# Six instead of four gate tiles in the half-size block of seven products

## The chip, the core and the metric

The kernel runs on one core of one Trainium2 chip. The time is that of the core on the device, in microseconds (us), as the median of several executions. One further execution is recorded by the hardware profiler; its span runs from the first to the last instruction. TensorE (PE) does the matmuls, VectorE (DVE), ScalarE (ACT) and GpSimd (POOL) the elementwise work; SyncE (SP) issues most DMA transfers.

## The reference

One layer of a hybrid encoder on 512 positions of width 2048, all in fp32:

```python
h = jnp.einsum('bsd,de->bse', x, w_in[layer])                 # 512 x 2048 by 2048 x 8192
qa, ka, va, ga, qb, kb, vb, gb = jnp.split(h, splits, axis=-1)  # 1024 columns each
ya = _dilated_attention(heads(qa, N_HEADS_A), heads(ka, N_HEADS_A), heads(va, N_HEADS_A), t5_bias)
yb = _neighbourhood_attention(heads(qb, N_HEADS_B), heads(kb, N_HEADS_B), heads(vb, N_HEADS_B), na_rpb[layer])
ya = merge(ya) * jax.nn.silu(ga.astype(jnp.float32))
yb = merge(yb) * jax.nn.silu(gb.astype(jnp.float32))
y = jnp.concatenate([ya, yb], axis=-1).astype(x.dtype)
out = jnp.einsum('bse,ed->bsd', y, w_out[layer])
x = _layer_norm(DEEPNORM_ALPHA * x + out, ln_gain[layer], ln_bias[layer])
```

Each group has 16 heads of 64. Group A sees keys at three dilations with a bucketed bias, group B a two-dimensional neighbourhood with its own bias. The gate paths `ga` and `gb` are 2 x 1024 columns: 16 gate tiles of 128 columns, one for each pair of heads.

## The kernel before, in words

**Precision.** Every fp32 operand is split into a high part (rounded to the type that TensorE takes at full rate, `wh` for a weight) and a low part (`wl`, the rest). A product is three matmuls: high by high, high by low, low by high. ScalarE makes the high half (an activation with Copy), VectorE the low half (a subtraction); a ring `halves` of six tiles holds three pairs, so splits run at most two units ahead of TensorE.

**Stage 1, projections.** First a plain block computes 4 gate tiles while x arrives (`plain_block`). Then `strassen_block` computes the six 1024-column projections k, q, v of the two groups, and, after the fourth of them, one more block of kind "s" with some gate tiles. Each of these blocks is a two-by-two block product done with seven products instead of eight (Strassen's method in a form with fewer additions). A product is a list of units; a unit has four steps: add two quarters of the weight where the product needs it (L371, VectorE), high half (L375, ScalarE), low half (L380, VectorE), matmuls. `run_blocks` issues for step n the addition of unit n+3, the high half of unit n+2, then the functions that hang `behind` this step (combining the products into results, storing, loading), the low half of unit n+2 and last the matmuls of unit n. The order on PE, DVE and ACT is the order in which the code is written; SP and POOL are ordered by a scheduler.

In a normal block the 1024 columns of weight are the moving operand, 512 at a time (L402 to L404). In the "s" block the weight tile is the stationary operand and 256 positions of x move (L393 to L395); the result has the gate's columns on partitions. Four quarters of the weight are loaded (`load`), four results combined (`combine_`, `last`) and passed through the gate function (`silu`: ScalarE tanh, VectorE closing) to DRAM (`sg_d`).

**Stage 2, attention.** 128 score steps n (four for each head, eight for each pair i = n // 8; pairs alternate between group A, even i, and group B, odd i). Step n does on PE: two score matmuls (L665, L666), then in two portions a number of *fillers*, and between the portions the transposes of step n-2's probabilities (L685). VectorE adds the bias and takes the maximum (L622), ScalarE exponentiates (L626); after the transposes ScalarE makes the high half `th` (L690) and VectorE the low half `tl` (L691). In every fourth step (n % 4 == 2) the eight value matmuls of the previous head (L707) read `th` and then `tl`; ScalarE copies one half (L831), VectorE adds (L832, `y`). For a pair, once in eight steps: the denominators are inverted (L843), transposed, copied by ScalarE (L720), sent to DRAM and loaded back spread over partitions as `rc` by POOL (L721, L723); six steps later VectorE multiplies by the gate (L730) and by `rc` (L738) and splits the result (L739, L740).

The **fillers** are independent matmuls that keep PE at work: first the plain gate tiles (`gate_unit`, 48 matmuls of 512 columns each, L561; each needs two weights of 128 x 1024, split in L546 and L547, and a closing L567), then the first half of the output projection (`out_first`, L755, 384 matmuls). A table gives how many fillers each of four consecutive steps takes; 49 are used before step 0, what is left is issued after the last step.

**Stage 3.** The second half of the output projection, the residual and the layer norm.

Of the kernel before, what the change touches and what calls it, by code (L numbers as in the profile page):

```python
# [25 lines left out]
HALF = 256  # L26
# [44 lines left out]
def hybrid_layer(tc, xT, xn, w_in, w_early, w_mid, w_gate, w_out, t5x, brow, rpb, cmask, eye, gain, lbias, out):  # L71
    nc = tc.nc
    from contextlib import ExitStack
    with ExitStack() as ctx:
# [19 lines left out]
        def slot(tag, dtype=F32, name=None):  # L94
            return arena.tile([128, sizes[tag[0]]], dtype, name=name or tag, tag=tag)
# [254 lines left out]
        def strassen_block(src, kind, g, hooks):  # L350

            base = len(jobs)
            units, tiles = (2, 1) if kind == "s" else (4, 2)

            def load(q, tags):
                def run():
                    for u in range(units):
                        raw = slot(tags[u], F32, "braw")
                        nc.sync.dma_start(raw, src[units * q + u])
                        raws[q].append(raw)  # L360
                return run
# [3 lines left out]
            def product(i, pool, q, other=None, onto=None):  # L365
                accs = [] if onto is None else onto
                first, skip = onto is None, onto is not None

                def add(u):
                    if other is not None:  # L370
                        nc.vector.tensor_tensor(raws[q][u], raws[q][u], raws[other][u], ALU.add)  # L371

                def high(u):
                    h = halves.next("wh", F32R)
                    nc.scalar.activation(h, raws[q][u], AF.Copy)  # L375
                    return h

                def low(u, h):
                    l = halves.next("wl", F32R)
                    nc.vector.tensor_tensor(l, raws[q][u], f(h), ALU.subtract)  # L380
                    return h, l

                def run(u, h, l):
                    if u == 0 and first:
                        accs.extend(bank(pool, "acc") for _ in range(tiles))
                    if kind == "s":
                        for kk in range(4):
                            k = 4 * u + kk
                            ah, al = operand(i, k)
                            for n in range(2):  # L390
                                c = slice(256 * kk + 128 * n, 256 * kk + 128 * n + 128)
                                o = accs[0][:, HALF * n:HALF * n + HALF]
                                nc.tensor.matmul(o, h[:, c], ah, start=first and k == 0 and n == 0, stop=False, skip_group_check=skip)  # L393
                                nc.tensor.matmul(o, h[:, c], al, start=False, stop=False, skip_group_check=skip)
                                nc.tensor.matmul(o, l[:, c], ah, start=False, stop=k == 7 and n == 1, skip_group_check=skip)  # L395
                    for t in range(2 if kind != "s" else 0):
                        for kk in range(2):
                            k = 2 * u + kk
                            ah, al = operand(i, k)
                            c = slice(512 * kk, 512 * kk + 512)  # L400
                            q = slice(128 * t, 128 * t + 128)
                            nc.tensor.matmul(accs[t], ah[:, q], h[:, c], start=first and k == 0, stop=False, skip_group_check=skip)  # L402
                            nc.tensor.matmul(accs[t], al[:, q], h[:, c], start=False, stop=False, skip_group_check=skip)  # L403
# [17 lines left out]
            def pair(name):  # L421
                if name not in made:
                    t = temps.next(name)
                    made[name] = [t[:, :512], t[:, 512:]]
                return made[name]

            p1 = product(1, pss, 0)
# [4 lines left out]
            product(3, None, 3, onto=p5)  # L432
            product(4, None, 0, 2, onto=p7)
            tags = list(sets)
            if kind == "s":
                for q, ahead, i, m in ((0, 6, 0, 0), (1, 5, 0, 2), (3, 3, 1, 0), (2, 0, 1, 2)):
                    behind.setdefault(base - ahead, []).append(load(q, tags[i][m:m + 2]))
            else:
                for q, ahead, i in ((0, 6, 0), (1, 4, 1), (3, 2, 2)):
                    behind.setdefault(base - ahead if base else -4, []).append(load(q, tags[i]))  # L440
                at(2, 2, load(2, tags[1]))

            def keep(t):
                nc.scalar.activation(pair("r1")[t], p1[t], AF.Copy)
# [27 lines left out]
            def put(name, ch, half, t):  # L472
                o = p1[t] if name == "c11" else pair(home[name])[t]
                if kind == "v":
                    store_v(g, ch, half, t, o)
                    return
                sg = vst.next("sg")[:, :512]
                silu(sg, o)
                for n in range(2):
                    nc.sync.dma_start(sg_d[EARLY + 2 * ch + n][:, HALF * half:HALF * half + HALF], sg[:, HALF * n:HALF * n + HALF])  # L480
# [324 lines left out]
        with tc.manual_schedule(engines=engines):  # L805
            prepare()
            for _ in range(3):
                close()
            while step[0] < 0:
                fill(7)  # L810
                close()
            for n in range(136):
                b, i = n % 4, n // 8
                mixing = n % 4 == 2 and 6 <= n <= 130
                amount = ((8, 6, 1, 6) if n < 64 else (8, 7, 1, 7))[b]
                if b == 0 and n < 124:
                    load_bias(n // 4 + 1)
                if n % 8 == 0 and n < 120:
                    load_kq(i + 1)
                if n % 8 == 4 and n < 128:  # L820
                    if n < 120:
                        load_v(i + 1)
                    load_sg(i)
                exponent = scores(n) if n < 128 else None
                while held:
                    held.pop(0)()
                if mixing:
                    if exponent:
                        exponent()
                    mine, theirs, y, t = values(n // 4 - 1)  # L830
                    nc.scalar.activation(t, theirs, AF.Copy)  # L831
                    nc.vector.tensor_tensor(y, mine, t, ALU.add)  # L832
# [185 lines left out]
def _weights(w_in, w_out):  # L1018
# [19 lines left out]
    mid = []  # L1038
    for i in range(2):
        for j in range(2):  # L1040
            a = np.concatenate([w[8 * i:8 * i + 8, :, c:c + 128] for c in gate[EARLY + 2 * j:EARLY + 2 * j + 2]], axis=2)
            mid.append(a.reshape(2, 4, 128, 256).transpose(0, 2, 1, 3).reshape(2, 128, 1024))
# [38 lines left out]
```

## Time and profile before

| | |
|---|---|
| time, median of 3 executions | 976.12 us (976.05 to 976.37) |
| profiled execution | 976.42 us, its span 974.6 us |
| granted TensorE clock | 0.996 of full speed on average |
| half-size block, in the span | 367.9 to 409.1 us |
| attention, first to last scores | 576.4 to about 870 us |

How to read a row: times are us from the span's start, first the start, then the duration; `wl<-braw,wh` means that tile wl is written from braw and wh; `x4` is a count of like instructions that a row merges; what stands in brackets at the end is how long the engine was idle before and what ended the wait. A row of windows has start:end, then for each engine the busy time with its count of instructions, the granted clock, the DMA engines' busy share and GB/s. In the page's slices each digit is a busy share in tenths.

### The profile page before, as it was taken

Reading aid. Unit: us, or ns where it says so; the run is one execution under the profiler, and the core shown is the slowest. Engines: PE = TensorE matmul, PEld = TensorE weight load, DVE = VectorE, ACT = ScalarE, POOL = GpSimd, SP = SyncE. Lnnn points to the kernel's source line nnn. Section 1 sums busy time; section 2 is a strip of 40 time slices with the busy share of each in tenths; the row PEclk is TensorE's granted clock in tenths of the full one; section 3 lists DMA queues with packets and bytes.
Section 4 is the critical chain, followed back from the end, with each engine's and each line's share of the span. In section 5 each row is a group of like instructions: output and inputs, shape, how many; then the busy total and the mean of one; then the engine's idle time right before and its main releaser. Section 6 shows DMA issues by size and latency. Waiting matters only on the chain.

```text
span 974.6 us, 13969 instructions
## 1 busy us (share of the span) xinstructions
PE 964.0 (99%) x4779; PEld 804.2 (83%) x4779; DVE 758.6 (78%) x1143; ACT 497.1 (51%) x858; POOL 176.5 (18%) x325
## 2 busy tenths in 40 slices
PE   8999999999999999999999999999999999999996
PEld 6887888888888889988888888888888888888885
DVE  7897778679789777796788856777876767777877
ACT  7454444444444344443445446767766666763300
POOL 1006646835642000000000000011110000100021
PEclk9999999999999999999999999999999999999998
DMA  9816796698496087420872687878877688768222
GB/s 332 280 65 133 225 329 213 171 308 220 115 334 226 22 283 204 163 96 21 265 183 96 205 273 213 226 224 228 233 229 222 195 236 214 203 223 298 87 72 102
DMA packets 119287, 194.17 MB, mean 199 GB/s; under 512 B 48479, under 2 KB 68831, under 8 KB 119216
## 3 DMA queue, kind: packets, MB, share of 16 engines
q1 hardware_dynamic: 106544, 169.67, 57.0%
q0 software_dynamic: 12096, 22.95, 8.7%
q8 instruction: 38, 0.62, 0.3%
q10 hardware_dynamic: 576, 0.66, 0.2%
q14 instruction: 33, 0.27, 0.1%
HBM read 148.68 MB, written 44.50 MB: 198 GB/s over the span
## 4 chain that ended last, share of the span: by engine, by line
PE 96%; DVE 1%; ACT 1%; DMA 1%; issue 0%; SPq 0%; DVEq 0%; ACTq 0%
PE acc L402 16%; PE acc L404 16%; PE acc L403 16%; PE acc L755 15%; PE acc L561 9%; PE pv L707 4%; PE pt L685 4%; PE sc L666 2%; PE sc L665 2%; PE pt L259 1%; PE acc L278 1%; PE acc L279 1%; PE acc L280 1%; PE sc L755 1%; PE acc L393 1%; PE acc L395 1%
## 5 line engine op out<-in xcount | busy, mean ns | idle before, releaser
L375 ACT ACTIVATE wh<-braw 128x1024 fp32r<-128x1024 f32 x182 | 193.3, 1062 | 268.6 <-PE acc L403 201.4
L380 DVE TENSOR_TENSOR wl<-braw,wh 128x1024 fp32r<-128x1024 f32 x182 | 222.7, 1226 | 52.4 <-ACT wh L375 52.1
L402 PE MATMUL acc<-wh,xk 128*128 128x512 f32 x384 | 151.5, 394 | 0.0
L404 PE MATMUL acc<-wl,xk 128*128 128x512 f32 x384 | 149.9, 390 | 0.0
L403 PE MATMUL acc<-wh,xk 128*128 128x512 f32 x384 | 149.7, 390 | 0.0
L371 DVE TENSOR_TENSOR braw<-braw 128x1024 f32<-128x1024 f32 x104 | 127.7, 1228 | 0.1
L402 PE MATMUL acc<-wh,op 128*128 128x512 f32 x288 | 113.3, 393 | 0.0
L404 PE MATMUL acc<-wl,op 128*128 128x512 f32 x288 | 112.3, 390 | 0.0
L403 PE MATMUL acc<-wh,op 128*128 128x512 f32 x288 | 112.2, 390 | 0.0
L755 PE MATMUL acc<-wh,yk 128*128 128x512 f32 x320 | 108.2, 402 | 0.0
L691 DVE TENSOR_TENSOR tl<-pt,th 128x256 fp32r<-128x256 f32 (+1 forms) x128 | 71.1, 555 | 35.8 <-ACT th L690 34.1
L690 ACT ACTIVATE th<-pt 128x256 fp32r<-128x256 f32 (+1 forms) x128 | 62.2, 489 | 47.6 <-PE pt L685 45.4
L404 PEld LDWEIGHTS acc<-wl,xk 128*128 128x128 f32 x384 | 72.1, 188 | 15.3
L402 PEld LDWEIGHTS acc<-wh,xk 128*128 128x128 f32 x384 | 72.2, 188 | 15.2 <-ACT bias L150 0.9
L403 PEld LDWEIGHTS acc<-wh,xk 128*128 128x128 f32 x384 | 72.2, 188 | 14.4
L626 ACT ACTIVATE p<-s,mn 128x512 f32<-128x512 f32 (+1 forms) x96 | 62.2, 648 | 29.0 <-DVE mn L622 28.6
L622 DVE CUSTOM_DVE_ANT_0 s<-sc,biases 128x512 f32<-128x512 f32 (+2 forms) x128 | 67.7, 529 | 10.9 <-PE sc L666 10.0
L561 PE MATMUL acc<-xk,wh 128*128 128x512 f32 x256 | 75.3, 404 | 0.0
L755 PEld LDWEIGHTS acc<-wh,yk 128*128 128x128 f32 x320 | 58.5, 189 | 8.8
L160 POOL DMA_DIRECT2D bias<-rows_d x128 | 61.3, 487 | 16.4 <-DMA bias<-rows_d 5.3
L755 PE MATMUL acc<-wl,yk 128*128 128x512 f32 x160 | 64.0, 403 | 0.0
L404 PEld LDWEIGHTS acc<-wl,op 128*128 128x128 f32 x288 | 54.1, 188 | 11.4
(185 smaller groups left out, 1707.1 us busy)
## 6 DMA issues: line engine op xcount, KB each, us to landing
braw<-in_w_in SPq DMA_DIRECT2D x96, 512.0 KB
wraw<-in_w_out SPq DMA_DIRECT2D x32, 512.0 KB
k_d<-kst SPq DMA_DIRECT2D x64, 128.0 KB
q_d<-kst SPq DMA_DIRECT2D x64, 128.0 KB
v_d<-vst SPq DMA_DIRECT2D x32, 256.0 KB
q<-q_d SPq DMA_DIRECT2D x32, 256.0 KB
wraw<-in_w_gate SPq DMA_DIRECT2D x16, 512.0 KB
k<-k_d SPq DMA_DIRECT2D x16, 512.0 KB
```

The lines of the kernel that those rows point to most:

```text
L371: nc.vector.tensor_tensor(raws[q][u], raws[q][u], raws[other][u], ALU.add)
L375: nc.scalar.activation(h, raws[q][u], AF.Copy)
L380: nc.vector.tensor_tensor(l, raws[q][u], f(h), ALU.subtract)
L402: nc.tensor.matmul(accs[t], ah[:, q], h[:, c], start=first and k == 0, stop=False, skip_group_check=skip)
L403: nc.tensor.matmul(accs[t], al[:, q], h[:, c], start=False, stop=False, skip_group_check=skip)
L404: nc.tensor.matmul(accs[t], ah[:, q], l[:, c], start=False, stop=k == 7, skip_group_check=skip)
L561: nc.tensor.matmul(acc, w[:, k * 128:k * 128 + 128], X[8 * u + k][:, s], start=u == 0 and n == 0 and k == 0, stop=u == 1 and n == 2 and k ...
L622: nc.vector.tensor_tensor_reduce(*flat, bias, 1.0, 3e38, ALU.add, ALU.min, mn)
L626: nc.scalar.activation(p[:, to:to + n].rearrange("p (b r c) -> p b r c", r=8, c=c), s[:, :n].rearrange(order, r=8, c=c), AF.Exp, bias=mn, ...
L690: nc.scalar.activation(th, pt[:, :nch], AF.Copy)
L691: nc.vector.tensor_tensor(tl, pt[:, :nch], f(th), ALU.subtract)
L755: nc.tensor.matmul(acc[:, part], yk[k][:, s, c], w[:, wk], start=first and kk == 0 and n == 0, stop=last and kk == 1 and n == 2)
```

## The change

Of the 16 gate tiles, 4 stay in the first plain block. The half-size block takes 6 instead of 4, and the fillers 6 instead of 8. In the half-size block a unit becomes 768 columns (two k-tiles of 384) where it was 1024 (four k-tiles of 256), each product has 4 units instead of 2, and its result takes two PSUM banks (512 and 256 columns) where it took one. Quarters are loaded and placed as in the normal blocks. The table of fillers goes from (8, 6, 1, 6) up to step 63 and (8, 7, 1, 7) after it to (6, 5, 1, 4) up to step 75 and (8, 6, 1, 6) after it.

```diff
-EARLY, MID = 4, 4
+EARLY, MID = 4, 6
...
-            units, tiles = (2, 1) if kind == "s" else (4, 2)
+            units, tiles = 4, 2
+            cols, wide = (128 * MID // 2, (512, HALF * (MID // 2 - 2))) if kind == "s" else (512, (512, 512))
...
-                        raw = slot(tags[u], F32, "braw")
+                        raw = slot(tags[u], F32, "braw")[:, :2 * cols]
...
                     if kind == "s":
-                        for kk in range(4):
-                            k = 4 * u + kk
+                        for kk in range(2):
+                            k = 2 * u + kk
                             ah, al = operand(i, k)
-                            for n in range(2):
-                                c = slice(256 * kk + 128 * n, 256 * kk + 128 * n + 128)
-                                o = accs[0][:, HALF * n:HALF * n + HALF]
+                            for n in range(MID // 2):
+                                c = slice(cols * kk + 128 * n, cols * kk + 128 * n + 128)
+                                o = accs[n // 2][:, HALF * (n % 2):HALF * (n % 2) + HALF]
...
-            if kind == "s":
-                for q, ahead, i, m in ((0, 6, 0, 0), (1, 5, 0, 2), (3, 3, 1, 0), (2, 0, 1, 2)):
-                    behind.setdefault(base - ahead, []).append(load(q, tags[i][m:m + 2]))
-            else:
-                for q, ahead, i in ((0, 6, 0), (1, 4, 1), (3, 2, 2)):
-                    behind.setdefault(base - ahead if base else -4, []).append(load(q, tags[i]))
-                at(2, 2, load(2, tags[1]))
+            for q, ahead, i in ((0, 6, 0), (1, 4, 1), (3, 2, 2)):
+                behind.setdefault(base - ahead if base else -4, []).append(load(q, tags[i]))
+            at(2, 2, load(2, tags[1]))
...
-                amount = ((8, 6, 1, 6) if n < 64 else (8, 7, 1, 7))[b]
+                amount = ((6, 5, 1, 4) if n < 76 else (8, 6, 1, 6))[b]
```

What moves on the engines, at three places. In the changed program the lines behind the first edits have other numbers: L394 to L396 are L393 to L395 of before, and from L480 on a line stands two lower. First PE at the first k-tile of the half-size block, before and after (acc is the PSUM bank, xk the moving half of x, wh and wl the weight's halves):

```order
L393 MATMUL acc_3306<-xk0_98,wh_3246 128x256
L394 MATMUL acc_3306<-xk0_98,wh_3246 128x256
L395 MATMUL acc_3306<-xk0_98,wl_3248 128x256
L393 MATMUL acc_3306<-xk0_98,wh_3246 128x256
L394 MATMUL acc_3306<-xk0_98,wh_3246 128x256
L395 MATMUL acc_3306<-xk0_98,wl_3248 128x256
```

```order
L394 MATMUL acc_3312<-xk0_98,wh_3250 128x256
L395 MATMUL acc_3312<-xk0_98,wh_3250 128x256
L396 MATMUL acc_3312<-xk0_98,wl_3260 128x256
L394 MATMUL acc_3312<-xk0_98,wh_3250 128x256
L395 MATMUL acc_3312<-xk0_98,wh_3250 128x256
L396 MATMUL acc_3312<-xk0_98,wl_3260 128x256
L394 MATMUL acc_3313<-xk0_98,wh_3250 128x256
L395 MATMUL acc_3313<-xk0_98,wh_3250 128x256
L396 MATMUL acc_3313<-xk0_98,wl_3260 128x256
```

Each k-tile of x now meets three weight tiles, the third in a second bank.

Next VectorE from the sum of head 2 (y) to the last low half of head 3, the cycle in which pair 0 is multiplied by rc, before and after:

```order
L832 TENSOR_TENSOR y<-pv,tmp 64x512
L691 TENSOR_TENSOR tl<-pt,th 128x256
L622 ISA s,mn<-sc,biases 128x192
L622 ISA mn 128x1
L691 TENSOR_TENSOR tl<-pt,th 128x256
L547 TENSOR_TENSOR wl<-wraw,wh 128x1024
L738 TENSOR_TENSOR y<-y,rc 128x512
L622 ISA s,mn<-sc,biases 128x512
L622 ISA mn 128x1
L691 TENSOR_TENSOR tl<-pt,th 128x256
L843 RECIPROCAL den<-den 128x8
```

```order
L830 TENSOR_TENSOR y<-pv,tmp 64x512
L689 TENSOR_TENSOR tl<-pt,th 128x256
L620 ISA s,mn<-sc,biases 128x192
L620 ISA mn 128x1
L689 TENSOR_TENSOR tl<-pt,th 128x256
L736 TENSOR_TENSOR y<-y,rc 128x512
L620 ISA s,mn<-sc,biases 128x512
L620 ISA mn 128x1
L689 TENSOR_TENSOR tl<-pt,th 128x256
L841 RECIPROCAL den<-den 128x8
```

The split of a filler's weight (wl) has left this cycle, so VectorE comes to the multiplication by rc one split earlier. In the same way the cycle of head 4 loses a gate closing (sgo).

Last SP in the steps 8 to 13, the transfers that are issued around the loading of rc for pair 0, before and after:

```order
L589 DMA ql<-q_d 64x2x512
L540 DMA wraw<-in_w_gate 128x1024
L649 DMA biases<-biasa_d 128x560
L598 DMA vv<-v_d 128x1024
L609 DMA sg<-sg_d 128x512
L540 DMA wraw<-in_w_gate 128x1024
```

```order
L587 DMA ql<-q_d 64x2x512
L538 DMA wraw<-in_w_gate 128x1024
L647 DMA biases<-biasa_d 128x560
L596 DMA vv<-v_d 128x1024
L607 DMA sg<-sg_d 128x512
```

The weight load that closed this group before has left it; the next transfer is a bias table of a later head.

More of the change, by code (lines that the diff above doesn't have):

```diff
@@ L384, in run @@
                     if u == 0 and first:
[L385 removed]
+                        accs.extend(bank(pool, "acc")[:, :n] for n in wide)
                     if kind == "s":
[L387 to L388 removed]
+                        for kk in range(2):
+                            k = 2 * u + kk
                             ah, al = operand(i, k)
[L390 to L393 removed]
+                            for n in range(MID // 2):
+                                c = slice(cols * kk + 128 * n, cols * kk + 128 * n + 128)
+                                o = accs[n // 2][:, HALF * (n % 2):HALF * (n % 2) + HALF]
+                                nc.tensor.matmul(o, h[:, c], ah, start=first and k == 0 and n % 2 == 0, stop=False, skip_group_check=skip)
                                 nc.tensor.matmul(o, h[:, c], al, start=False, stop=False, skip_group_check=skip)
[L395 removed]
+                                nc.tensor.matmul(o, l[:, c], ah, start=False, stop=k == 7 and (n % 2 == 1 or n == MID // 2 - 1),
+                                                 skip_group_check=skip)
                     for t in range(2 if kind != "s" else 0):
@@ L476, in put @@
                     return
-                sg = vst.next("sg")[:, :512]
+                sg = vst.next("sg")[:, :wide[t]]
                 silu(sg, o)
-                for n in range(2):
-                    nc.sync.dma_start(sg_d[EARLY + 2 * ch + n][:, HALF * half:HALF * half + HALF], sg[:, HALF * n:HALF * n + HALF])
+                for n in range(wide[t] // HALF):
+                    nc.sync.dma_start(sg_d[EARLY + MID // 2 * ch + 2 * t + n][:, HALF * half:HALF * half + HALF], sg[:, HALF * n:HALF * n + HALF])
             for t in range(tiles):
```

11 lines of the change are left out of this document (6 added, 5 removed).

## The prediction

> **What bounds the kernel now.** I read the page first, then the groups of instructions by form, then the order of time at two places, and last the waits.
>
> ```profile
> PE 964.0 (99%) x4779; PEld 804.2 (83%) x4779; DVE 758.6 (78%) x1143; ACT 497.1 (51%) x858; POOL 176.5 (18%) x325
> PE   8999999999999999999999999999999999999996
> PEclk9999999999999999999999999999999999999998
> ...
> PE 96%; DVE 1%; ACT 1%; DMA 1%; issue 0%; SPq 0%; DVEq 0%; ACTq 0%
> ```
>
> TensorE is busy for 99% of the span, in every slice, at the full granted clock, and the chain that ended last is 96% TensorE. So the change is worth first of all what it takes from or adds to TensorE's instruction stream, and a stall counts only if it reaches TensorE. A busy share can hide short waits, because the page says that ends of matmuls are modelled. I therefore price matmuls by the distance between starts, not by their duration.
>
> ```profile
> 403.83 0.28 PE L394 MATMUL acc<-xk,wh 128*128 128x256 f32 x1
> 403.95 0.28 PE L395 MATMUL acc<-xk,wl 128*128 128x256 f32 x1
> 404.07 0.28 PE L393 MATMUL acc<-xk,wh 128*128 128x256 f32 x1
> ...
> 367.90:409.10 41.20, 41.20 (x346) 41.20 (x345) 30.89 (x34) 18.42 (x22) 0.00 (x0) 1.00 0.64 192
> ```
>
> In the half-size block one matmul of 256 columns starts 0.12 us after the last. The window of the whole block (columns: TensorE, weight load, DVE, ACT, POOL, clock, DMA share, GB/s) holds its 336 of them and some transposes in 41.2 us, at most 0.1226 us each.
>
> ```profile
> 620.77 1.09 PE L561 MATMUL acc<-xk,wh 128*128 128x512 f32 x4
> 621.69 0.60 PE L685 MATMUL pt<-ident,p 128*128 128x128 f32 x4
> ...
> 576.88 1.98 PE L561 MATMUL acc<-xk,wh 128*128 128x512 f32 x8
> 578.70 0.39 PE L665 MATMUL sc<-k,q 128*128 128x512 f32 x1
> ```
>
> Fillers of 512 columns start 0.92/4 = 0.23 us apart between attention steps (the row's two decimals allow 0.225 to 0.235), and 1.82/8 = 0.2275 us in a longer row.
>
> **The change, part by part.**
>
> *TensorE, removed.* Two gate tiles fewer among the fillers: 2 units x 3 passes x 8 = 48 matmuls each, 96 in all, at 0.23 us: -22.1 us (-21.6 at 0.225, -22.6 at 0.235).
>
> *TensorE, added.* The half-size block had 7 products x 8 k-tiles x 2 tiles x 3 = 336 matmuls and gets 7 x 8 x 3 x 3 = 504: 168 more at 0.12 us, +20.2 us (at 0.1226 us, +20.6). Net -1.9 us, between -2.4 and -1.0. The seven products save one multiplication in eight, and much of that is eaten by 256 columns costing 0.12 us and not half of 0.2275.
>
> [...]
>
> *VectorE and ScalarE in the half-size block.* A unit shrinks from 24 to 18 matmuls, so from 24 x 0.12 = 2.9 to 18 x 0.12 = 2.16 us, with 768 columns to be added and split in it.
>
> ```profile
> L380 DVE TENSOR_TENSOR wl<-braw,wh 128x1024 fp32r<-128x1024 f32 x182 | 222.7, 1226 | 52.4 <-ACT wh L375 52.1
> L375 ACT ACTIVATE wh<-braw 128x1024 fp32r<-128x1024 f32 x182 | 193.3, 1062 | 268.6 <-PE acc L403 201.4 <-issue 29.0 <-PE acc L394 19.3
> L88 DVE TENSOR_TENSOR kst<-pt,kst 128x512 fp32r<-128x512 f32 x16 | 11.1, 691 | 16.0 <-ACT kst L87 16.0
> ```
>
> 768 columns on VectorE lie midway between 0.691 and 1.226: 0.96 us. A unit with an addition takes 2 x 0.96 = 1.92 of 2.16 us. Over the block: 28 splits and 16 additions make 42.2 us, the five combining operations and four gate closings, each on 512 and on 256 columns, about 10 us: 52 of 60.5 us, 86% against 30.89/41.2 = 75% now. The tightest place is the start of the fifth product: after the last matmul of the fourth, three combining operations on 512 columns (2.1 us) and a split stand in 2.16 us, then three on 256 columns, a gate closing and a split (about 2.9 us) in the next. Counted from the fifth product's start, the second of these splits is done at about 5.7 us, and its matmuls begin at three units, 6.5 us. Cover 0.8 us, since splits run two units ahead. Cost 0; if the cover were gone, both steps together exceed their 4.3 us by at most 1.6 us. The loads become 16 of 384 KB (6.3 MB for 4.2) in a block that is 20 us longer; the DMA share was 0.64, so 0.
>
> *Attention with fewer fillers.* Up to step 75 the fillers go from 21 (23 from step 64) to 16 in four steps: 454 - 353 = 101 fewer, 23 us less of TensorE's time; later 21 for 23, and 46 instead of 15 are left at step 128, behind which the tail has more cover than now.
>
> ```profile
> 577.10:750.60 173.50, 173.49 (x943) 144.30 (x942) 128.42 (x303) 120.10 (x284) 17.88 (x33) 1.00 0.81 226
> ```
>
> VectorE's 128.4 us lose four splits and two gate closings (4 x 1.2 + 2 x 0.7 = 6.3): 122 in 150 us, 81% instead of 74%; ScalarE 76%, from 69%. The mean fits. Single cycles of four steps might not, because TensorE is 5 x 0.23 = 1.15 us earlier at the next value products (L707), which need VectorE's last low half (tl). The fullest cycle now:
>
> ```profile
> 619.04 0.69 DVE L832 TENSOR_TENSOR y<-pv,tmp 64x512 f32<-64x512 f32 x1 [1.02 <-ACT tmp L831]
> 620.38 0.68 DVE L567 SCALAR_TENSOR_TENSOR sgo<-sgo,acc 128x512 f32<-128x512 f32 x1
> 622.18 1.22 DVE L547 TENSOR_TENSOR wl<-wraw,wh 128x1024 fp32r<-128x1024 f32 x1
> 624.53 0.68 DVE L730 TENSOR_TENSOR y<-y,sg 128x512 f32<-128x512 f32 x1
> 625.74 0.69 DVE L691 TENSOR_TENSOR tl<-pt,th 128x512 fp32r<-128x512 f32 x1
> ...
> 626.93 0.39 PE L707 MATMUL pv<-tl,vv 128*128 128x512 f32 x1
> ```
>
> VectorE runs there without a gap from 619.04 to 626.43, 0.5 us before TensorE reads tl. With the same work, 1.15 us less would stall TensorE by 0.65 us. But in the changed order the gate closing (sgo, 0.6 us) is no longer in this cycle, which leaves about nothing. Over a whole pair of group A there is more room:
>
> ```profile
> 615.10:635.10 20.00, 19.99 (x109) 16.29 (x108) 15.63 (x35) 15.38 (x35) 2.17 (x4) 1.00 0.82 217
> 635.10:650.70 15.60, 15.60 (x86) 13.03 (x86) 11.44 (x33) 10.74 (x30) 2.16 (x4) 1.00 0.84 237
> ```
>
> 15.6 of 20.0 us in the first of these stretches (group A) become about 15.0 of 17.7, 85%; the group-B stretch behind it goes from 73% to some 80%. The other cycles have one or two extras in the changed order, not three. Cost 0, bound 0.65 us in each of the nine cycles of group A, about 6 us.
>
> *What is late next: rc.* The reciprocals of the denominators go by ScalarE and POOL to DRAM and back, and VectorE waits for them in order.
>
> ```profile
> 600.23 0.25 ACT L720 ACTIVATE tmp<-pt 8x128 f32<-8x128 f32 x1
> 600.88 0.54 POOL L721 DMA_DIRECT2D rc_d<-tmp  x1 [21.50 <-ACT tmp L720]
> 605.78 0.38 SPq L540 DMA_DIRECT2D wraw<-in_w_gate  x1
> 605.83 1.07 POOL L723 DMA_DIRECT2D rc<-rc_d  x2 [3.83 <-DMA rc_d<-tmp]
> 613.42 0.69 DVE L738 TENSOR_TENSOR y<-y,rc 128x512 f32<-128x512 f32 x1 [0.58 <-DMA rc<-rc_d]
> 616.39 0.42 DVE L691 TENSOR_TENSOR tl<-pt,th 128x256 fp32r<-128x256 f32 x1 [0.66 <-ACT th L690]
> 616.87 0.64 PE L707 MATMUL pv<-tl,vv 128*128 128x256 f32 x4
> ...
> 636.06 0.25 ACT L720 ACTIVATE tmp<-pt 8x128 f32<-8x128 f32 x1
> 647.81 0.67 DVE L738 TENSOR_TENSOR y<-y,rc 128x512 f32<-128x512 f32 x1
> ...
> 673.45 0.53 POOL L721 DMA_DIRECT2D rc_d<-tmp  x1 [8.90 <-ACT tmp L720]
> 685.85 0.69 DVE L738 TENSOR_TENSOR y<-y,rc 128x512 f32<-128x512 f32 x1 [0.17 <-DMA rc<-rc_d]
> ...
> DMA to landing us min/median/max: 2.9/5.3/7.3
> ```
>
> For pair 0 rc lands 613.42 - 600.48 = 12.9 us after the ScalarE copy ended (pair 4: 12.7, counting 0.3 us to POOL), for pair 2 after at most 11.5 us, since nothing waited. At best it is the second load's issue (half of the 1.07 us behind 605.83, so 5.9 us) and the fastest landing of 2.9 us: 8.8. From VectorE's multiplication to the end of the tl behind it are 3.4 us, and TensorE reads it at 16.4 us now; ten fillers fewer on that stretch make it 14.1 us. So rc landing after 10.7 us stalls TensorE: 0 at 8.8, 2.2 us at 12.9. That can happen for the four group-A pairs with an even number up to step 75 (the others have longer steps behind them): 0 to 8.8 us. In the changed order the weight load that went out just ahead of rc (605.78 in pair 0) moves to other places, and POOL issues rc right behind rc_d, so I take it nearer to the early end: two of four late by 0.6 us, +1.2 us.
>
> *Sum.* -22.1 + 20.2 + 1.2 = -0.7 us. The profiled execution took 976.42 us, so 975.7; it lies 0.3 us above the median of 976.12, so 975.4 us by the median.
>
> **Rivals.**
>
> *A: nothing stalls.* -1.9 us, 974.2 us. For it: VectorE's work fits each cycle by the rows above, and TensorE is busy for 173.49 of 173.50 us there. Against: VectorE waited for rc three times already, and the stretch gets 14% shorter.
>
> [...]
>
> *B: rc becomes the bound of these stretches.* If the transfers take as long as in pair 0 for all four pairs, 4 x 2.2 = 8.8 us: 976.1 - 1.9 + 8.8 = 983 us. It turns the result to slower from a mean of about 1 us for each pair, a landing at 11.7 us. For it: pairs 0 and 4 show 12.9 and 12.7 us, and the same bytes have to pass in less time. Against: pair 2's 11.5 at most, with no wait.
>
> *C: VectorE bounds the half-size block and the full cycles.* 1.6 us in the block and 0.65 us in some three cycles: 976.1 - 1.9 + 3.5 = 977.7 us. Against it: idle time that the cycles still have, and 0.8 us of cover.
>
> **How the numbers follow.** What this kernel's measurement can tell from no change is 0.2%, 2 us: below 974.2 is faster, above 978.1 slower. My forecast, some stalls that eat a part of the gain: 0.50. A: 0.25, half of which falls below 974.2, as the net of TensorE alone reaches to -2.4 us. B 0.15, of which most is slower; C 0.10, a third of it slower. I add a little to faster, as the pace of removed fillers may be higher than I see: faster 0.20, same 0.62, slower 0.18. The range goes from 973.7 (-2.4, no stall) to 979.0 us (four late rc of 1.2 us each), which leaves the worse half of B out.
>
> **What would show it.** The window of the half-size block should be 61 to 62 us, its matmuls still 0.12 us apart; if longer, look whether wl or wh ended a wait of TensorE there (C). The stretch from the first scores to step 76 should shrink from 173.5 to 150-152 us with VectorE at 80%; gaps between L707 starts at the th-to-tl change show stalls, and VectorE's idle time before the multiplication by rc says whether it is rc. If rc's wait grows from 2.1 us in total to over 8, B holds. The forecast is wrong if the block or the next block's start shows waits for braw, or if fillers wait for a weight.

## The result, and the profile after

The changed kernel takes 991.38 us in the median (990.34 to 992.54, 4 executions), the kernel before on the same chip 976.23 us (976.05 to 976.37). The ratio is 1.0155, with an interval of 1.0143 to 1.0167: 1.5% slower. The forecast was 975.4 us and the range ended at 979.0. The profiled execution took 991.0 us with a span of 989.2 us, 14.6 us longer than before.

The page of the changed kernel: busy time, TensorE in 40 slices, and the chain that ended last, by engine and by line.

```profile
PE 966.9 (98%) x4851; PEld 805.7 (81%) x4851; DVE 767.3 (78%) x1168; ACT 504.7 (51%) x871; POOL 185.5 (19%) x323
PE   8999999999999999999999999989997999999996
...
PE 21%; issue 4%; DMA 3%; DVE 1%; ACT 1%; POOL 0%; DVEq 0%; ACTq 0%; POOLq 0%
PE acc L753 13%; PE pv L705 2%; PE pt L683 2%; DMA rc_d<-tmp 2%; DMA rc<-rc_d 1%; PE sc L753 1%; PE pt L753 1%; PE sc L664 1%; PE sc L663 1%; POOL rc L721 0%; DVE s L620 0%; DVE z L939 0%; DVE wl L545 0%; ACT p L624 0%; ACT wh L544 0%
```

Two of the slices that were all 9 are an 8 and a 7 now, at 643 to 668 and at 742 to 767 us. The shares of the chain add up to about 30%, so it follows only the last part of the span, and in that part the two transfers that bring `rc` now stand in it.

The windows of the half-size block and of the stretch from the first scores to step 76 (columns as in the prediction: TensorE, weight load, DVE, ACT, POOL, clock, DMA share, GB/s). The second has the same place in the program as the window 577.10:750.60 of before.

```profile
367.40:428.50 61.10, 61.10 (x510) 60.97 (x509) 49.70 (x63) 29.10 (x40) 0.00 (x0) 1.00 0.54 167
597.60:762.80 165.20, 154.77 (x842) 125.82 (x841) 121.86 (x298) 116.09 (x279) 17.79 (x33) 0.99 0.83 222
```

The block is as forecast: 61.1 us (61 to 62 were expected), without a gap on TensorE, VectorE at 49.7 us (52 expected). The attention stretch is not: it should have shrunk from 173.5 to 150 to 152 us and takes 165.2. VectorE's work in it is 121.9 us, what I had counted (122), but TensorE is idle for 165.20 - 154.77 = 10.4 us where it was idle for 0.01.

What TensorE waited for in the attention of the changed kernel, from 590 to 870 us (us in total, times, the longest). The same view of the attention before is empty.

```profile
PE pt L714 <- DVE den L841: 5.9, 3, 3.5
PE pv L705 <- ACT th L688: 4.5, 8, 1.2
```

And VectorE's wait for `rc` over the whole execution, after and then before:

```profile
DVE y L736 <- DMA rc<-rc_d: 9.0, 4, 4.7
```

```profile
DVE y L738 <- DMA rc<-rc_d: 2.1, 3, 1.3
```

By the test that the prediction set ("from 2.1 us in total to over 8") rival B holds. But TensorE does not wait for the low half behind `rc`, as rival B had it. It waits for denominators. The worst place, in order of time, first TensorE and then VectorE:

```profile
750.92 0.40 PE L753 MATMUL acc<-wl,yk 128*128 128x512 f32 x1
754.82 0.27 PE L714 MATMUL pt<-ident,den 128*8 128x128 f32 x1 [3.51 <-DVE den L841]
...
756.55 2.07 PE L705 MATMUL pv<-th,vv 128*128 128x512 f32 x4 [1.22 <-ACT th L688]
758.42 1.56 PE L705 MATMUL pv<-tl,vv 128*128 128x512 f32 x4
759.82 0.39 PE L753 MATMUL acc<-wh,yk 128*128 128x512 f32 x1
```

```profile
753.00 0.69 DVE L736 TENSOR_TENSOR y<-y,rc 128x512 f32<-128x512 f32 x1 [4.66 <-DMA rc<-rc_d]
753.61 0.35 DVE L620 CUSTOM_DVE_ANT_0 s<-sc,biases 128x192 f32<-128x192 f32 x1
...
753.88 0.69 DVE L689 TENSOR_TENSOR tl<-pt,th 128x512 fp32r<-128x512 f32 x1
754.49 0.19 DVE L841 RECIPROCAL den<-den 128x8 f32<-128x8 f32 x1
```

VectorE stands for 4.66 us before the multiplication of pair 7 by `rc` (L736). Queued behind it are a bias addition with maximum, a low half, and the reciprocal of pair 8's denominators (L841). TensorE comes to the transpose of those denominators (L714) 3.51 us too early, has to wait for the reciprocal, and can issue none of the fillers behind it.

How late `rc` was, from ScalarE, POOL and VectorE (above) together:

```profile
733.92 0.25 ACT L718 ACTIVATE tmp<-pt 8x128 f32<-8x128 f32 x1
```

```profile
734.47 0.53 POOL L719 DMA_DIRECT2D rc_d<-tmp  x1 [7.36 <-ACT tmp L718]
742.65 1.06 POOL L721 DMA_DIRECT2D rc<-rc_d  x2 [7.66 <-DMA rc_d<-tmp]
```

The 4 KB of `rc_d` needed about 8 us, the two loads of `rc` up to 10 more: 753.00 - 734.17 = 18.8 us from the ScalarE copy to the multiplication, against the 12.9 us that was the longest in my prediction. By the same reading pair 1 took 15.8 us. These two pairs are exceptions: from the end of the ScalarE copy to the landing of the later load, the first ten pairs took 11.3 us on average before and 11.7 us after, but pair 1 went from 8.3 to 15.7 us and pair 7 from 10.9 to 18.7 us.

**The ledger.** The span should have changed by -1.9 us and changed by +14.6: 16.5 us were lost. I add up, over the attention, all distances between successive matmul starts above 0.34 us, less 0.23 us for each. Before that is 0.3 us, after 14.6 us: 6.8 ahead of the denominators' transposes, 4.3 ahead of the first value product (L705, for the most part waiting for `th`), 1.5 between value products, 1.4 in value products that start 0.43 us apart from 756.55 on, 0.7 at scores. Of the 4.3 us, 1.3 stand right behind the worst wait (the row 756.55). At most some 9.4 us (6.8 + 1.3 + 1.4, rounded) are thus in `rc`'s wake, some 5 us are not.

### The profile page after: what moved, and what is told of

It reads as the page before. It is cut to its first block, busy times and chain, and to the rows that moved or that the text cites. A ratio compares the mean times of both kernels' runs of the same rounds, so it can differ in the third digit from the quotient of the medians.

```text
span 989.2 us, 14203 instructions
## 1 busy us (share of the span) xinstructions
PE 966.9 (98%) x4851; PEld 805.7 (81%) x4851; DVE 767.3 (78%) x1168; ACT 504.7 (51%) x871; POOL 185.5 (19%) x323
## 5 line engine op out<-in xcount | busy, mean ns | idle before, releaser
L376 ACT ACTIVATE wh<-braw 128x1024 fp32r<-128x1024 f32 (+1 forms) x196 | 202.1, 1031 | 278.3 <-PE acc L405 209.0
L381 DVE TENSOR_TENSOR wl<-braw,wh 128x1024 fp32r<-128x1024 f32 (+1 forms) x196 | 232.8, 1189 | 59.7 <-ACT wh L376 59.5
L372 DVE TENSOR_TENSOR braw<-braw 128x1024 f32<-128x1024 f32 (+1 forms) x112 | 132.0, 1179 | 0.0
L753 PE MATMUL acc<-wh,yk 128*128 128x512 f32 x320 | 110.5, 402 | 0.0
L620 DVE CUSTOM_DVE_ANT_0 s<-sc,biases 128x512 f32<-128x512 f32 (+2 forms) x128 | 67.5, 527 | 8.5 <-PE sc L664 7.9
L405 PEld LDWEIGHTS acc<-wh,op 128*128 128x128 f32 x288 | 54.1, 188 | 11.0
```

The lines of the kernel that those rows point to most:

```text
L620: nc.vector.tensor_tensor_reduce(*flat, bias, 1.0, 3e38, ALU.add, ALU.min, mn)
L753: nc.tensor.matmul(acc[:, part], yk[k][:, s, c], w[:, wk], start=first and kk == 0 and n == 0, stop=last and kk == 1 and n == 2)
```

## The experiments

The ratio behind each time is to the kernel before on the same chip. Its median was 975.9 to 977.2 us there, so differences of about 1 us between runs on different chips are not read.

**Is the new block the cause, or the thinner table?** The kernel before, with its four tiles in the half-size block, gets only the new table. Since it has 96 fillers more, they are left to the end and issued there in portions of eight.

```diff
-                amount = ((8, 6, 1, 6) if n < 64 else (8, 7, 1, 7))[b]
+                amount = ((6, 5, 1, 4) if n < 76 else (8, 6, 1, 6))[b]
...
-            fill(400)
+            for _ in range(24):
+                fill(8)
+                close()
```

> The kernel before with only the table of fillers of the change, (6, 5, 1, 4) up to step 75 and (8, 6, 1, 6) after it; the fillers that are left over, some 140, are issued after the last step. Block, gate tiles and TensorE's work are as before. If the thinner table alone makes the stalls: 976 + 13 to 17 = 989 to 993 us. If the larger half-size block or the moved transfers make them: 975 to 979 us.

993.72 us, ratio 1.0172 (1.0152 to 1.0192), slightly above the span expected of the table. TensorE's waits in its attention (575 to 848 us) and then behind it, where the leftovers are issued:

```profile
PE pv L707 <- ACT th L690: 4.3, 8, 1.7
PE pt L716 <- DVE den L843: 1.1, 2, 0.9
```

```profile
PE acc L755 <- DVE wl L547: 3.3, 1, 3.3
```

With the old block, the table alone makes TensorE wait for `th` and for denominators, where it never waited; VectorE's wait for `rc` in the attention is 4.9 us there, against 0.8 before. By the same sum over the starts this is 7.9 us in the attention; another 7.7 us are lost in the leftovers, which stand for this kernel alone, so its time agrees with the expectation partly for another reason. The other 6.7 of the changed kernel's 14.6 us answer to the worst wait with its wake (3.7 + 1.3 + 1.4 = 6.4 us). This kernel does not have that wait: its two gate tiles more go on as fillers there, and its pair 7 was multiplied at 724.2 us without a wait. So the table alone is enough for half the loss, and the rest needs the table together with the rest of the change. That it is the gate tiles' earlier end among the fillers is argued and not shown: the new block with the old table was not run.

**What is `rc` worth?** The changed kernel without the round trip of `rc` (a tile of ones takes its place).

```diff
+        ones = slot("n10", F32, "ones")
+        nc.gpsimd.memset(ones, 1.0)
...
-                nc.gpsimd.dma_start(rc_d[i], row)
-                for a in range(2):
-                    nc.gpsimd.dma_start(rc[64 * a:64 * a + 64], _view(rc_d, 1024 * i + 512 * a, [[0, 64], [1, 512]]))
-                rcs[i] = rc
+                rcs[i] = ones
```

> The changed kernel with the round trip of rc left out: the copy of the reciprocals to DRAM and their loading back are not issued, and VectorE multiplies by a tile of ones that was set before attention (so the result is not normalised; all else, the transposes and the multiplication included, stays). Theory 1 (the late rc holds VectorE, and behind it the reciprocal of the next pair, for which TensorE's transposes wait): the waits go, 991.4 falls by 9 to 13 us, to about 978 to 982 us; what is left over 974.2 is waits of the value products for th. Theory 2 (VectorE and ScalarE have too little time in the shorter cycles of four steps; rc is only where it shows): hardly changed, 987 us or more.

981.05 us, ratio 1.0043 (1.0026 to 1.0059): 10.3 us less than the changed kernel (10.9 by the ratios). The denominators' wait is gone from the view; what is left in the attention:

```profile
PE pv L708 <- ACT th L691: 2.0, 6, 0.6
```

By the same sum over the starts 4.6 us are left in its attention, 10.0 less. So the round trip of `rc` carries about two thirds of the loss. Half of the wait for `th` went with it.

**Is it the lateness, or the place in VectorE's order?** All transfers stay; the multiplication by `rc` and the two halves behind it come two steps later, so that the next pair's reciprocal goes first.

```diff
-            later(0, lambda: nc.vector.tensor_tensor(y, y, rcs[i], ALU.mult), True)
-            later(1, lambda: nc.scalar.activation(t[:, 0], y, AF.Copy, scale=0.5))
-            later(2, lambda: nc.vector.scalar_tensor_tensor(t[:, 1], y, 0.5, f(t[:, 0]), op0=ALU.mult, op1=ALU.subtract), True)
+            later(2, lambda: nc.vector.tensor_tensor(y, y, rcs[i], ALU.mult), True)
+            later(3, lambda: nc.scalar.activation(t[:, 0], y, AF.Copy, scale=0.5))
+            later(4, lambda: nc.vector.scalar_tensor_tensor(t[:, 1], y, 0.5, f(t[:, 0]), op0=ALU.mult, op1=ALU.subtract), True)
```

> The changed kernel with the multiplication by rc and the split behind it two steps later (nothing left out). It is then held to the step of the value products, behind the reciprocal of the next pair, and rc has about 4 us more to land. Theory 1: nearly as without the round trip, 978 to 983 us; in the trace the wait of VectorE for rc falls from 9.0 us to under 2 and PE's wait for den to nothing. Theory 2: 987 us or more.

982.53 us, ratio 1.0056 (1.0040 to 1.0073): 8.9 of the 10.3 us come back without one byte less to move. No wait for `rc` is left in the attention, nor for a denominator, though `rc` is no earlier: that of pair 7 landed 18.2 us after the copy (18.7 in the changed kernel), and the first ten took 13.2 us on average. So it is the place in VectorE's order that made the lateness cost TensorE time. The waits for `th` stay:

```profile
PE pv L705 <- ACT th L688: 3.7, 4, 1.1
```

**Why is `rc` late?** The changed kernel loads only four of its filler weights and splits these four again and again; every split and matmul stays; the other loads of filler weights are left out.

```diff
-                raws.append(raw_ring.next("wraw"))
-                nc.sync.dma_start(raws[-1], stream.pop(0))
+                if len(kept) < 4:
+                    kept.append(raw_ring.next("wraw"))
+                    nc.sync.dma_start(kept[-1], stream[0])
+                raws.append(kept[used[0] % 4])
+                used[0] += 1
+                stream.pop(0)
```

> The changed kernel with the weights of the fillers loaded four times only; the later splits read the same four tiles again (so gates and the first half of the output projection have wrong weights; splits, matmuls and rc are as before). About 12 MB of 512 KB transfers leave the stretch of attention. If rc is late because it queues behind the other transfers: rc lands earlier, its wait goes from 9.0 us to under 3, and the time falls to 978 to 984 us. If the round trip through DRAM and POOL is long by itself: 988 us or more.

980.50 us, ratio 1.0046 (1.0030 to 1.0062), as good as without `rc` at all. First VectorE's wait for `rc`, then the window of the attention from 596 to 756 us:

```profile
DVE y L741 <- DMA rc<-rc_d: 0.3, 1, 0.3
```

```profile
596.00:756.00 160.00, 157.19 (x864) 128.64 (x863) 123.40 (x302) 117.52 (x283) 17.76 (x33) 1.00 0.67 190
```

With a DMA share of 0.67 instead of 0.83, the same round trip is in time: pair 7's landed 14.4 us after the copy, and the first ten took 10.5 us on average. `rc` is late because of the other transfers, and not because of its own length or of POOL, which at the worst place issued `rc_d` 0.3 us after the copy. How the transfers hold each other up inside the DMA engines no run here shows.

**Which transfers stand in its way?** The rows of the changed kernel showed one suspect. SP's queue, in order of time:

```profile
724.11 0.42 SPq L607 DMA_DIRECT2D sg<-sg_d  x1
730.57 0.33 SPq L860 DMA_DIRECT2D gain<-in_lbias  x1
730.99 0.38 SPq L647 DMA_DIRECT2D biases<-biasa_d  x1
```

SP issued nothing for 6 us, while a load of a norm vector (L860) waited for the store of the last gate tile, and then seven transfers within 4 us, just ahead of pair 7's `rc`. (The kernel before has the same wait of SP, 6.5 us, and lost nothing by it.) The next kernel exchanges two slots, so that this load has another slot to wait for.

```diff
-        sg_out, sg_ring, rc_ring, y_ring = Ring("n6"), Ring("n8", "n9"), Ring("n10", "n11"), Ring("n5", "n7")
+        sg_out, sg_ring, rc_ring, y_ring = Ring("n10"), Ring("n8", "n9"), Ring("n6", "n11"), Ring("n5", "n7")
```

> The changed kernel with two buffers exchanged: the fillers' gate output takes a slot of the rc ring and the other way round (nothing left out). SP's queue then no longer holds, in the middle of attention, the load of a norm vector that waits for the last gate tile's store, and the bias, key and query loads behind it. If that blocked queue is what bunches the transfers of steps 64 to 75 and delays rc of pair 7: 4 to 6 us less, 985 to 988 us. If rc of pair 7 is late whatever stands in SP's queue: 990 to 992 us.

986.43 us, ratio 1.0102 (1.0082 to 1.0122), 5 us less, as expected. Yet the reason given for it does not hold. SP's rows now:

```profile
724.27 0.42 SPq L607 DMA_DIRECT2D sg<-sg_d  x1
730.06 0.32 SPq L647 DMA_DIRECT2D biases<-biasa_d  x1
```

The load has left the place, but the bias table behind it (L647) goes out at 730.06 us, only 0.9 us earlier than before (730.99), since it has a wait of its own. The waits for `rc` and for the denominators became shorter:

```profile
DVE y L736 <- DMA rc<-rc_d: 5.2, 6, 2.5
```

```profile
PE pt L714 <- DVE den L841: 2.5, 2, 1.6
```

The stalls in the attention are 9.9 us instead of 14.6. That the long wait at pair 7 is gone is shown (0.7 us are left, and its `rc` landed 14.8 us after the copy); which transfer made way for its `rc` is not.

**The rest.** About 5 us are left without `rc`. One more shift, on top of the later multiplication: the multiplication by the gate (L728) goes from step 4 to step 5 of the eight, where a value product takes VectorE's extras.

```diff
-                if n >= 8 and n % 8 == 4:
+                if n >= 8 and n % 8 == 5:
```

> As with the multiplication by rc two steps later, and the multiplication by the gate one step later, so that it too is held to the step of the value products (nothing left out). Theory 1 with VectorE's chain as the second cause: 0.6 us less in each of the nine to ten cycles in which a gate multiplication stands before the last low half, so 2 to 4 us below the run with rc alone, 975 to 980 us. If ScalarE, not VectorE, makes th late: no different from rc alone.

979.85 us, ratio 1.0028 (1.0016 to 1.0041), at the upper end of what was expected. With the exchanged slots on top:

> The changed kernel with rc two steps later, the gate multiplication one step later and the buffers exchanged (nothing left out). What is left over TensorE's own 974.2 are then only waits of the value products for th: 975 to 978 us. If the exchange does nothing: 979 to 981 us, as without it.

979.72 us, ratio 1.0034 (1.0023 to 1.0044). The expected further gain did not come: once the multiplication stands later, the exchange is worth nothing that can be measured. In this kernel's trace one of the waits that are left can be followed. VectorE, ScalarE and TensorE in order of time:

```profile
635.63 0.69 DVE L689 TENSOR_TENSOR tl<-pt,th 128x512 fp32r<-128x512 f32 x1 [0.55 <-ACT th L688]
636.24 0.68 DVE L738 SCALAR_TENSOR_TENSOR yk<-y,yk 128x512 fp32r<-128x512 f32 x1
636.84 1.22 DVE L545 TENSOR_TENSOR wl<-wraw,wh 128x1024 fp32r<-128x1024 f32 x1
637.97 0.68 DVE L620 CUSTOM_DVE_ANT_0 s<-sc,biases 128x512 f32<-128x512 f32 x1
```

```profile
638.76 0.72 ACT L624 ACTIVATE p<-s,mn 128x512 f32<-128x512 f32 x1 [1.97 <-DVE mn L620]
...
639.48 0.57 ACT L688 ACTIVATE th<-pt 128x512 fp32r<-128x512 f32 x1
```

```profile
639.06 0.40 PE L664 MATMUL sc<-k,ql 128*128 128x512 f32 x1
640.11 1.20 PE L705 MATMUL pv<-th,vv 128*128 128x512 f32 x4 [0.66 <-ACT th L688]
```

Two extras on VectorE (the low half of a finished pair and that of a filler's weight, 1.7 us from 636.24 to 637.97) stand ahead of a bias addition with maximum (L620). ScalarE's exponential waits 1.97 us for that maximum, and the high half `th` stands behind the exponential on ScalarE. So at this place the value products wait for VectorE by way of ScalarE, though their `pt` was there in time.

Two attempts to take this away. First, more fillers for group A, whose steps are the fuller ones, and fewer for group B, four-step sums 18 and 13 instead of 16:

```diff
-                amount = ((6, 5, 1, 4) if n < 76 else (8, 6, 1, 6))[b]
+                amount = ((6, 6, 1, 5) if n < 76 and i % 2 == 0 else (5, 4, 1, 3) if n < 76 else (8, 6, 1, 6))[b]
```

> The same with the fillers up to step 75 given out by group: (6, 6, 1, 5) in steps of group A, (5, 4, 1, 3) in steps of group B, instead of (6, 5, 1, 4) in both. If the remaining waits come from VectorE's and ScalarE's fuller cycles in group A: 1 to 2 us below the run without it, 974 to 976 us, at or under the kernel before. If group B has no room to give: 1 to 2 us above it.

982.98 us, ratio 1.0073 (1.0057 to 1.0089), 3.3 us worse than with the even table, where 1 to 2 us were expected if group B has no room to give. The waits for `th` fell from 2.0 to 1.4 us, and scores that wait for VectorE's addition `y` are new (0.9 us). That fits, but it is not all: of the 2.6 us between the profiled executions, 1.6 us stand behind the last scores by the sum over the starts, and this table also gives out seven fillers fewer up to step 75 (31 instead of 32 in eight steps). Second, the two extras held until the step of the value products, or two steps longer:

```diff
-            later(2, lambda: nc.vector.tensor_tensor(l, raw, f(h), ALU.subtract), True)
+            k = 2
+            while 4 <= step[0] < 64 and (step[0] + k) % 4 != 1:
+                k += 1
+            later(k, lambda: nc.vector.tensor_tensor(l, raw, f(h), ALU.subtract), True)
...
-            later(4, lambda: nc.vector.scalar_tensor_tensor(t[:, 1], y, 0.5, f(t[:, 0]), op0=ALU.mult, op1=ALU.subtract), True)
+            later(6 if i < 7 else 4, lambda: nc.vector.scalar_tensor_tensor(t[:, 1], y, 0.5, f(t[:, 0]), op0=ALU.mult, op1=ALU.subtract), True)
```

> The changed kernel with the three shifts (979.7 us), and in addition the low half of a filler's weight held until the step of the value products, and the low half of a finished pair two steps later, so that neither stands on VectorE ahead of a maximum that the exponential waits for. If the waits of the value products for the high half that are left (2.0 us in that kernel) come from VectorE work that happens to lie ahead of the maximum, 976.5 to 978.5 us and these waits below 1 us. If the shorter cycle itself is too tight for the chain from scores through maximum, exponential and transposes to the high half, no change: 979 to 981 us.

978.58 us, ratio 1.0035 (1.0023 to 1.0046), the same as the kernel without the hold (1.0034). The waits in the attention:

```profile
PE sc L666 <- DVE y L833: 1.4, 2, 0.7
PE pv L708 <- ACT th L691: 1.1, 3, 0.5
```

The wait for `th` is nearly halved (2.0 to 1.1 us, where the first theory had below 1), and a new one is there: scores wait for the bank that VectorE's addition `y` has still to read. The distances between TensorE's starts lose 4.3 us in all, against 4.8 without the hold. The wait that was followed above, near 640 us, is gone. So the work ahead of the maximum is one cause of the single waits, but where it goes instead, something else is late. The time lies between the two expectations and does not tell them apart.

**The control.** The kernel before with the same three shifts and its own table:

> The kernel before, with its own table of fillers and its own half-size block, and the three shifts of the last kernels: the multiplication by rc and its split two steps later, the gate multiplication one step later, the two slots exchanged. If these shifts only help where TensorE has to wait, this kernel has nothing to gain: 976 us, within 1 us of before. If they bring something of their own, whatever the table (a gain that I would then have credited to the mending of the stalls), it falls to 973 us or below.

975.20 us, ratio 0.9991 (0.9981 to 1.0000): no gain outside the bound of 0.2%. The shifts bring something only where TensorE has stalls. None of these kernels beats the kernel before.

## Why the prediction was wrong, by its steps

**TensorE, removed and added: right.** The block's window grew by 61.10 - 41.20 = 19.9 us for +20.2. From the scores of step 0 to those of step 8, where nothing stalls, are 17.78 us before (576.43 to 594.21) and 15.52 us after (596.93 to 612.45): 2.26 us for ten fillers fewer, 0.226 each (0.23 assumed). The rate of the rounded halves in the kernel before: their 512 columns start 0.23 us apart, while the four matmuls of 33 rows by 512 columns on fp32 tiles that are not rounded (L149, from 72.52 us) start (1.89 - 0.59) / 3 = 0.43 us apart. With no stall the kernel would stand about where rival A had it, 974.2 us: the profiled execution of the last changed kernel, 979.2 us, less its 4.3 us of stalls gives 974.9.

**The block's cover: right.** No wait of TensorE in it, cost 0 as taken.

**"What is late next: rc": the failing step.** It was put at +1.2 us, with a bound of 8.8. The runs give 10.3 us for the changed kernel with `rc` against the one without. Three things were wrong in that step:

- *The reader.* I followed VectorE's order from the multiplication by `rc` to the low half `tl` and stopped. The order that stands ahead of the prediction shows the reciprocal (L841) four rows behind the multiplication. TensorE's denominator transposes wait for it, and the kernel with a later multiplication got 8.9 us back by that order alone.
- *The pairs.* I excluded the odd ones, "the others have longer steps behind them". Pairs 1 and 7 were the two worst (2.1 and 4.7 us of VectorE's wait). Of the even pairs, 0 and 4 were late, as assumed ("two of four"), by 0.6 and 1.7 us; only pair 4 reached TensorE, again by a denominator. That their number came out is luck, since pair 0 stalled nothing.
- *The landing.* The longest I allowed was that of pair 0, 12.9 us, and I had looked at three of the sixteen pairs (pairs 5 and 10 of the kernel before landed after 13.3 us, where nothing waited). In the shorter stretch two pairs took 15.8 and 18.8 us. "The same bytes have to pass in less time" stood in the prediction as a point for rival B, and I set no price on it. The kernel with fewer weight loads shows that the other transfers made the difference. Whether it is the shorter time or the way they bunch is open: the stretch moved 222 GB/s, against 226 before.

Pair 7's two loads had landed some 10 us after 742.65 us, where the first was issued, in a stretch whose DMA share is 1.03 (the last section's window).

**Attention with fewer fillers: the cost 0 was wrong, its bound nearly right by luck.** "The mean fits" was true: 121.9 us of VectorE's work for 122. "Single cycles might not" was bounded at 6 us by `tl` behind VectorE's extras. About 5 us were lost, but most of it ahead of `th`, and where one such wait was followed, by way of the maximum and the exponential. I had checked one chain through the cycle, the longest on VectorE, and not the one that crosses from VectorE to ScalarE and back to TensorE.

**The rivals.** B named the right cause and had 0.15; its 983 us was still 8 us short, since it had the wrong reader and left out the other waits. With C's cycles beside it, 974.2 + 10.3 + 5 = 989.5 us, of a median of 991.4; the other 2 us are the part of the ledger (16.5 against 14.6) that no distance above 0.34 us shows, and stay unassigned. To take the rivals as exclusive was part of the mistake, since both start from the thinner table: the table takes five fillers, 1.15 us, from every four steps, while the rest of VectorE's and ScalarE's work and the attention's transfers stay.

## What to carry to other kernels

Where an engine in order waits for a transfer, price the wait by everything queued behind it until each thing's reader on the bounding engine, not by the next known reader; a small operation such as the reciprocal here (0.19 us) can be the one that hurts. When independent work is taken out from between dependent steps, the stretch gets shorter but most of its transfers stay (39.2 MB in 173.5 us before, 36.7 MB in 165.2 us after). A round trip that was just in time at a DMA share of 0.8 should then be priced with a landing longer than any now in the trace: here the average hardly moved, and two of ten landings cost most of the time. A mean busy share of 80% on the other engines says little about the chain that crosses them within one cycle.

## What the runs showed of the hardware that I had not expected

**Transfers.** The window of the changed kernel ahead of the worst wait (columns as above):

```profile
732.00:756.00 24.00, 19.37 (x108) 15.52 (x107) 14.56 (x34) 14.93 (x34) 1.59 (x3) 1.00 1.03 228
```

The DMA share is 1.03 there, at 228 GB/s, so the engines count as full; in the whole stretch they moved 222 GB/s at a share of 0.83. So 0.83 is an average over full and emptier pieces. Pair 7's two loads, in a full piece, took 8.7 and 9.7 us from issue to landing, while the median in the whole stretch was 4.3 us. The share does not measure bytes: the changed kernel moved 297 GB/s at a share of 0.97 from 648.00 to 650.40 us, and 219 GB/s at 1.05 from 752.00 to 754.80 us (the rows below).

**The clock.** Windows of the changed kernel, first a gap of 1.58 us and what follows it, then the worst gap and the time of the lower clock behind it:

```profile
648.00:650.40 2.40, 0.81 (x6) 0.37 (x5) 2.40 (x7) 1.42 (x4) 0.00 (x0) 1.00 0.97 297
650.40:654.40 4.00, 3.38 (x18) 2.70 (x19) 3.01 (x8) 3.02 (x10) 1.10 (x2) 1.00 0.72 180
...
752.00:754.80 2.80, 0.00 (x0) 0.01 (x1) 1.80 (x6) 0.80 (x3) 0.00 (x0) 1.00 1.05 219
...
756.02:759.43 3.41, 2.88 (x7) 2.30 (x8) 2.77 (x5) 1.72 (x6) 0.53 (x1) 0.50 0.50 121
```

Behind TensorE's idle time of 3.51 us the granted clock is 0.50 for 3.4 us: the four value products from 756.55 to 758.42 start 0.47 us apart on average, where 0.23 is usual. The kernel before with the new table shows it again, behind the 3.3 us for which its leftovers waited:

```profile
863.50:867.00 3.50, 0.35 (x2) 0.00 (x0) 3.01 (x5) 0.00 (x0) 0.00 (x0) 0.91 1.06 370
867.20:872.80 5.60, 5.60 (x13) 4.44 (x14) 3.81 (x6) 0.00 (x0) 0.00 (x0) 0.50 1.00 314
```

Here it lasts 6.8 us (866.4 to 873.2); in the 5.6 us shown, 13 matmuls took the time of 24. These two stalls thus cost more than their length: by the sum over the starts, 1.4 us on top of 3.7 in the changed kernel, and some 3 us on top of 3.5 here. Behind the gap of 1.58 us the clock stayed at 1.00. The kernel with the exchanged slots shows the lower clock without a gap as long as these two:

```profile
696.70:700.10 3.40, 1.42 (x7) 0.64 (x5) 2.58 (x8) 2.39 (x5) 0.57 (x1) 1.00 1.01 255
700.10:703.50 3.40, 3.19 (x13) 3.01 (x14) 3.18 (x6) 2.42 (x7) 0.56 (x2) 0.50 0.35 101
```

There TensorE had a gap of 1.60 us and soon after it one of 0.59 us, which ended at 700.31 us, and the clock was 0.50 for the 3.4 us from 700.1 us on. In the 3.4 us before, TensorE was busy for 1.42 us. So the clock can be lower without a single gap of 3.3 us ahead of it; how much idle time is enough these runs do not settle.
